# One hybrid decoder layer on one core: eight gate tiles placed in other groups of the SSD stage

## The chip, the cores and the metric

The kernel runs on 1 core of a Trainium2 chip, in one launch. The metric is device time in microseconds; a lower one is better. TensorE does the matmuls into PSUM, VectorE and ScalarE the elementwise work, GpSimd small copies, and SyncE and ScalarE issue the DMAs, each in its own order.

## The reference, cut to what matters

A layer takes 512 prompt tokens and 64 sample tokens (8 streams of 8), makes one wide input projection, and runs three branches whose outputs are merged with gates:

```python
hn = _rmsnorm(x, norm_g)
proj = hn @ w_in
u, v, gate_a, z, xbc, dt_raw, q, gate_x, merge = jnp.split(proj, _split_points(IN_SIZES), axis=-1)
...
h_a = u * _gmlp_spatial(v, w_spatial, b_spatial) * jax.nn.silu(gate_a)
xbc, conv_new = _causal_conv(xbc, conv0, conv_w, conv_b)
xs, bm, cm = jnp.split(xbc, [D_INNER, D_INNER + SSD_GROUPS * SSD_STATE], axis=-1)
...
y, h_new = _ssd(xh, dt, a, bm, cm, h0)      # chunks of 128 tokens, 8 groups of 4 heads
h_b = _gated_group_rmsnorm(y + xh * d_skip, z, ssd_norm_g)
...
m = g_a * (h_a @ w_proj_a) + g_b * (h_b @ w_proj_b) + g_x * (h_x @ w_proj_x)
return x + m @ w_out, ...
```

`gate_a` has 1024 channels, 8 tiles of 128. It is used only in branch A, which comes after the SSD stage.

## The kernel before, in words

All activations lie with channels on the partitions and the 576 tokens along the free dimension, in two halves of 288. Every float32 matmul is made of three fp32r terms: a weight block is split (`wsplit`, L100 and L101: a cast on ScalarE, a subtraction on VectorE) into `whi` and `wlo`, and `gemm_half` (L169) runs hi x hi, hi x lo and lo x hi over 8 blocks of channels, 24 matmuls of 288 columns for one tile and half, into one of four accumulators in PSUM.

The SSD stage works on 8 groups. A **job** is one tile of a projection with three parts: `load` (a DMA of weights on SyncE, two jobs ahead, into one of two slots of 1 MB), `prep` (the split, one job ahead), and `half(f)` for the two halves. One half with what follows it is called a **unit** here. The kinds of job:

- `conv_job(g, ci)`: a tile of xBC of group g; after its second half come the four taps of the convolution and SiLU on VectorE and ScalarE (L414 to L442).
- `z_job(g, j)`: z's two tiles of group g; tanh on ScalarE into a tile `th` of two buffers (L472), a product on VectorE into `zs` (L473), which has one buffer.
- `gate_job(jj)`: tile jj of `gate_a`; tanh (L743), product (L744) into a tile of its own that borrows a buffer of another name (`xs`, `raw`, `cacc`, `C`), and one store of 288 KB to `g_scr` by ScalarE's queue (L746). Weights are loaded for two tiles at once.
- `proj_job(r, p)`: branch B's output projection over a quarter of h_b.

Between the units stand the **steps** of the group whose convolutions were done a group before: twelve lists 0 to 11 of small matmuls and what goes with them (`steps`). Step 0 has the scores C·B of chunk 0 (`chunk_cb`, L541, L542), `start_y`, `decays(g, 2)` and the transposes of chunk 1 (`chunk_a`, L512); step 1 chunk 1's scores, the state of chunk 0 (`state`, L576, L582, L583) and, for the group before, `y_smp` (L614) and `gate_y` (L694 to L696 and the split into `qq`); step 3 chunk 2's scores, `y_off` (L601), `y_diag` (L557) of chunks 0 and 1, `decays(g, 3)` and `norm_y` of the group before (L708 to L711, L714); step 4 a state, `chunk_a(g, 3)` and `decays(g, 4)`; step 5 scores, `y_off` and `chunk_a(g, 4)`; step 8 the `y_diag` of chunks 2 and 3; step 9 that of the sample chunk and the transposes and updates of the sample states (`h0_T`, L653, L655; `h0_new`, L662, L667, L668); step 10 two `h0_T` and `c_h0` (L683); step 11 two `h0_new` and `c_h0`. `decays` loads a chunk's cumulative sums by a broadcast DMA into `e`, which has three buffers (L498), adds a mask on VectorE (L499) and takes exponentials on ScalarE (L501). All small results go through three PSUM buffers (`s_tile`).

`PLACES` says after which unit of its group each step stands; a place behind the group's last unit falls into the next group. `decays(g + 1, 0)` and `(g + 1, 1)` stand three units before the group's end, `chunk_a(g + 1, 0)` after its last unit, `conv_out(g + 1)` (eight small stores on ScalarE's queue, L450 to L454) after the next group's unit 3 or, from group 2 on, after the last unit.

TensorE's order is just the order of this list. The other engines' orders are set when the program is built, by a scheduler with costs of its own; each engine then works in order and waits for semaphores.

Before, groups 0 and 1 have 6 jobs, group 2 and all others 8; group 7, which has no next group, has gate tiles 0 to 3 where the others have convolutions. Tiles 4 to 7 follow in a tail with the last `y_smp`, `gate_y` and `norm_y`, then `proj_job(3, p)`.

Of the kernel before, what the change touches and what calls it, by code (L numbers as in the profile page):

```python
# [8 lines left out]
F32 = mybir.dt.float32  # L9
# [3 lines left out]
ALU = mybir.AluOpType  # L13
# [4 lines left out]
P = 128  # L18
D = 1024
KD = D // P  # L20
TP = 512
TS = 64
T = TP + TS
# [5 lines left out]
G = 8  # L29
# [4 lines left out]
TW = TP + 192  # L34
EPS = 1e-6
O_U, O_V, O_GA, O_Z, O_XBC, O_DT, O_Q, O_GX, O_M = 0, 1024, 2048, 3072, 5120, 9216, 9248, 9760, 10272
# [6 lines left out]
def tile_hybrid_step(  # L43
# [8 lines left out]
    V, S, PE, GP, SY = nc.vector, nc.scalar, nc.tensor, nc.gpsimd, nc.sync  # L52
# [3 lines left out]
    w_in2 = w_in[0]  # L56
# [7 lines left out]
    g_scr = dpool.tile([P, KD, T], F32, name="g_scr")  # L64
# [62 lines left out]
    def load_block(src, r0, nk, cols):  # L127

        raw = rpool.tile([P, 2048], F32, tag="wraw", name="wraw").rearrange("p (k c) -> p k c", k=nk)
        o = 0  # L130
        for c0, n in cols:
            SY.dma_start(out=raw[:, :, o:o + n],
                         in_=src[r0:r0 + nk * P, c0:c0 + n].rearrange("(k p) c -> p k c", p=P))
            o += n
        return raw

    def wsplit(raw, nk, o, n=P, e=None):
        hi = ws["pool"].tile([P, 1024], F32R, tag="whi", name="whi")[:, 0:nk * n].rearrange("p (k c) -> p k c", k=nk)
        lo = ws["pool"].tile([P, 1024], F32R, tag="wlo", name="wlo")[:, 0:nk * n].rearrange("p (k c) -> p k c", k=nk)
        split(raw[:, :, o:o + n], hi, lo, e)  # L140
        return hi, lo
# [48 lines left out]
    with ExitStack() as stb:  # L190
        banks(stb, 4, 1, 3)
        ws["pool"] = stb.enter_context(tc.tile_pool(name="wb", bufs=2))
        pb = stb.enter_context(tc.tile_pool(name="pb", bufs=1))
# [27 lines left out]
        for tiles in ((0, 1, 2), (3, 4)):  # L221
# [12 lines left out]
            w = 3 * P if n == 3 else P + TS  # L234
            for k in range(KD):
                ps = s_tile()
# [3 lines left out]
                g = gcol[:, k:k + 1]  # L240
# [480 lines left out]
        def gate_job(jj):  # L721

            k = {}

            def load():
                if jj % 2 == 0:
                    gate_th["w", jj // 2] = load_block(w_in2, 0, KD, [(O_GA + jj * P, 256)])

            def prep():
                k["w"] = wsplit(gate_th["w", jj // 2], KD, (jj % 2) * P)  # L730

            def half(f):
                if f == 0:
                    if jj < 3:
                        if jj == 0:
                            gate_th["x"] = pb.tile([P, 3, TW], F32, tag="xs", name="thx", bufs=2)
                        gate_th[jj] = gate_th["x"][:, jj, 0:T]
                    else:
                        tag, nb = (("raw", 2), ("raw", 2), ("cacc", 2), ("cacc", 2), ("C", 2))[jj - 3]
                        gate_th[jj] = pb.tile([P, T], F32, tag=tag, name="thm", bufs=nb)  # L740
                ps, sl = gemm_half(k["w"], KD, xh, xl, f)
                th = pb.tile([P, HT], F32, tag="th", name="th", bufs=2)
                S.activation(th, ps, AF.Tanh, scale=0.5)  # L743
                V.scalar_tensor_tensor(gate_th[jj][:, sl], th, 1.0, ps, ALU.add, ALU.mult)  # L744
                if f == 1:
                    S.dma_start(out=g_scr[:, jj], in_=gate_th[jj])  # L746
            return Job(load, prep, half)

        def proj_job(r, p):
# [25 lines left out]
        with tc.manual_schedule(engines={mybir.EngineType.PE}):  # L775
            def group_jobs(g):

                c = [conv_job(g + 1, ci) for ci in range(4)] if g + 1 < G else [gate_job(0), gate_job(1), gate_job(2), gate_job(3)]
                z = [z_job(g, 0), z_job(g, 1)]
                if g == 0:  # L780
                    return [z[0], *c, z[1]]
                if g == 1:
                    return [c[0], c[1], z[0], c[2], c[3], z[1]]
                if g == 2:
                    return [c[0], c[1], z[0], z[1], c[2], proj_job(0, 0), c[3], proj_job(0, 1)]
                p = [proj_job(g // 2 - 1, 2 * (g % 2) + i) for i in range(2)]
                a, b = (p, z) if g % 2 else (z, p)
                return [c[0], a[0], c[1], a[1], c[2], b[0], c[3], b[1]]

            def yd(g, *cs):  # L790
                y_add(g, cs, y_diag(g, cs))

            def steps(g):

                w = [[] for _ in range(12)]
                w[0] = [lambda: chunk_cb(g, 0), lambda: start_y(g), lambda: decays(g, 2), lambda: chunk_a(g, 1)]
                w[1] = [lambda: chunk_cb(g, 1), lambda: state(g, 0)]
                if g > 0:
                    w[1] += [lambda: y_smp(g - 1), lambda: gate_y(g - 1)]
                w[2] = [lambda: state(g, 1), lambda: chunk_a(g, 2)]  # L800
                w[3] = [lambda: chunk_cb(g, 2), lambda: y_off(g, 1), lambda: yd(g, 0, 1), lambda: decays(g, 3)]
                if g > 0:
                    w[3] += [lambda: norm_y(g - 1)]
                w[4] = [lambda: state(g, 2), lambda: chunk_a(g, 3), lambda: decays(g, 4)]
                w[5] = [lambda: chunk_cb(g, 3), lambda: y_off(g, 2), lambda: chunk_a(g, 4), lambda: h0_load(g, 0)]
                w[6] = [lambda: state(g, 3), lambda: chunk_t4(g), lambda: h0_load(g, 1)]
                w[7] = [lambda: y_off(g, 3), lambda: chunk_cb(g, 4)]
                w[8] = [lambda: yd(g, 2, 3), lambda: state_out(g), lambda: h0_T(g, 0, 0)]
                w[9] = [lambda: yd(g, 4), lambda: h0_T(g, 0, 1), lambda: h0_new(g, 0, 0), lambda: h0_new(g, 0, 1)]
                w[10] = [lambda: c_h0(g, 0), lambda: h0_T(g, 1, 0), lambda: h0_T(g, 1, 1)]  # L810
                w[11] = [lambda: h0_new(g, 1, 0), lambda: h0_new(g, 1, 1), lambda: c_h0(g, 1)]
                return w

            halves = [(j, h) for j in (conv_job(0, ci) for ci in range(4)) for h in range(2)]
            between = {}

            def put(u, *fs):
                between.setdefault(u, []).extend(fs)  # L820

            put(7, lambda: decays(0, 0), lambda: decays(0, 1))
            PLACES = {0: (3, 4, 5, 6, 7, 8, 9, 10, 11, 12, 13, 14), 1: (1, 3, 4, 5, 6, 7, 8, 9, 10, 12, 13, 14),
                      2: (1, 3, 4, 5, 6, 7, 8, 9, 10, 11, 12, 13)}
            for g in range(G):
                u0 = len(halves)
                halves += [(j, h) for j in group_jobs(g) for h in range(2)]
                n = len(halves) - u0
                if g == 0:
                    put(u0 + 2, lambda: chunk_a(0, 0), lambda: conv_out(0))  # L830
                else:

                    between[u0 - 1] = between.get(u0 - 1, []) + [lambda g=g: chunk_a(g, 0)]
                w = steps(g)
                at = PLACES.get(g, (0, 1, 2, 4, 5, 7, 8, 9, 10, 12, 13, 14))
                for i, a in enumerate(at):
                    put(u0 + a, *w[i])
                if g + 1 < G:
                    put(u0 + n - 3, lambda g=g: decays(g + 1, 0), lambda g=g: decays(g + 1, 1))
                    put(u0 + n + (3 if g < 2 else -1), lambda g=g: conv_out(g + 1))  # L840
            units = []
            for u, x in enumerate(halves):
                units += [x, (None, between.get(u, []))]
            tail = {0: [lambda: y_smp(G - 1), lambda: gate_y(G - 1)], 4: [lambda: norm_y(G - 1)]}
            for i, u in enumerate([(j, h) for j in (gate_job(jj) for jj in range(4, 8)) for h in range(2)]):
                units += [u, (None, tail.get(i, []))]
            units += [(j, h) for j in (proj_job(3, p) for p in range(4)) for h in range(2)]

            jobs = [u[0] for u in units if u[0] is not None and u[1] == 0]
            at = {id(j): i for i, j in enumerate(jobs)}  # L850
            jobs[0].load()
            jobs[0].prep()
            jobs[1].load()
            for j, h in units:
                if j is None:
                    for w_ in h:
                        w_()
                    continue
                i = at[id(j)]
                if h == 0:  # L860
                    if i + 2 < len(jobs):
                        jobs[i + 2].load()
                    if i + 1 < len(jobs):
                        jobs[i + 1].prep()
                j.half(h)
# [651 lines left out]
```

## Time and profile before

| | |
|---|---|
| median of 3 runs | 1118.99 us (1118.35 to 1119.67) |
| the profiled execution | 1120.8 us |
| its span, first to last instruction | 1119.1 us |
| TensorE, VectorE, ScalarE, GpSimd busy | 1088.0, 797.0, 628.6, 25.0 us |
| group 0 (its units in the trace) | 62.01 to 109.73 us |
| group 1 | 109.73 to 168.44 us |
| group 2 | 168.44 to 240.97 us |
| groups 3 to 6 | 240.97 to 505.10 us |
| group 7 | 505.10 to 570.19 us |

The limits of the groups are the starts of the first matmul of their first job. A row of the timeline gives start, duration, engine, line, operation, tiles and shapes, and in brackets how long the engine had been idle and what ended that. A matmul's row lasts longer than the distance to the next one, since matmuls are pipelined.

### The profile page before, as it was taken

What the parts mean: (1) busy time and instruction counts of PE and PEld (TensorE: products, weight loads), DVE (VectorE), ACT (ScalarE), POOL (GpSimd) and SP (SyncE); (2) the same over time, 40 slices, a digit from 0 to 9 for tenths busy, and PEclk for the clock granted to TensorE, in tenths of its full rate; (3) what the DMA queues carried; (4) which work ended last, traced back from release to release, by engine and by line L of the source; (5) the groups of instructions that cost most, each with busy time, mean ns of one, the idle gap of its engine ahead of it and who ended that gap; (6) DMA issues with size and microseconds to landing.
All of it is one profiled execution on the core that took longest, in us unless ns stands there. A gap on an engine that the chain in (4) does not pass through costs nothing. (4 is left out here: it accounts for less than half of the span.)

```text
span 1119.1 us, 20422 instructions
## 1 busy us (share of the span) xinstructions
PE 1088.0 (97%) x8152; PEld 1010.9 (90%) x8152; DVE 797.0 (71%) x1468; ACT 628.6 (56%) x1303; POOL 25.0 (2%) x109
## 2 busy tenths in 40 slices
PE   5999999999999999999999999999999999999997
PEld 3999889999999999999999777899999998889776
DVE  4779797868677886877644765899965567765743
ACT  6366686777767576775543345365643235565421
POOL 1010000000000000000000000000000000000000
PEclk9999999999999999999999999999999999999999
DMA  6343535344553525445235525744642543556311
GB/s 172 108 112 111 149 112 148 101 140 109 153 144 110 135 90 149 112 146 161 97 103 178 184 70 167 252 156 160 207 147 97 175 144 113 151 160 211 138 47 76
DMA packets 163214, 153.82 MB, mean 137 GB/s; under 512 B 10472, under 2 KB 141584, under 8 KB 163120
## 3 DMA queue, kind: packets, MB, share of 16 engines
q1 hardware_dynamic: 138288, 130.32, 38.4%
q10 hardware_dynamic: 24832, 22.21, 6.0%
q8 instruction: 64, 1.05, 0.4%
q14 instruction: 30, 0.25, 0.1%
HBM read 128.32 MB, written 24.18 MB: 136 GB/s over the span
## 5 line engine op out<-in xcount | busy, mean ns | idle before, releaser
L169 PE MATMUL acc<-hn_hi,whi 128*128 128x288 f32 x896 | 270.2, 302 | 0.2 <-DVE zs L473 0.2
L169 PE MATMUL acc<-hn_lo,whi 128*128 128x288 f32 x896 | 264.2, 295 | 0.0
L169 PE MATMUL acc<-hn_hi,wlo 128*128 128x288 f32 x896 | 264.1, 295 | 0.0
L169 PEld LDWEIGHTS acc<-hn_hi,whi 128*128 128x128 f32 x896 | 168.2, 188 | 2.3 <-issue 1.2
L169 PEld LDWEIGHTS acc<-hn_lo,whi 128*128 128x128 f32 x896 | 168.4, 188 | 0.4
L169 PEld LDWEIGHTS acc<-hn_hi,wlo 128*128 128x128 f32 x896 | 168.1, 188 | 0.1
L934 PE MATMUL acc<-hn_hi,w 128*128 128x288 f32 x640 | 110.1, 299 | 0.0
L934 PE MATMUL acc<-tT,w 128*128 128x288 f32 x720 | 107.0, 298 | 0.0
L100 ACT CAST w<-wraw 128x1024 fp32r<-128x1024 f32 x64 | 58.1, 916 | 87.0 <-PE acc L934 28.3
L101 DVE TENSOR_TENSOR wlo<-wraw,whi 128x1024 fp32r<-128x1024 f32 x72 | 87.9, 1221 | 23.0 <-ACT whi L100 22.3
L169 PE MATMUL acc<-hb,whi 128*128 128x288 f32 x512 | 104.2, 298 | 0.0
L934 PEld LDWEIGHTS acc<-tT,w 128*128 128x128 f32 x720 | 98.1, 188 | 1.2 <-issue 0.9
L100 ACT CAST whi<-wraw 128x1024 fp32r<-128x1024 f32 x72 | 75.6, 1050 | 41.6 <-PE acc L169 39.3
L934 PEld LDWEIGHTS acc<-hn_hi,w 128*128 128x128 f32 x640 | 92.5, 188 | 1.9 <-DVE thx L952 0.5
L428 DVE SCALAR_TENSOR_TENSOR cacc<-raw,cwh,cacc 128x600 f32<-128x600 f32 x96 | 80.5, 838 | 3.6 <-ACT cacc L426 2.7
L169 PEld LDWEIGHTS acc<-hb,whi 128*128 128x128 f32 x512 | 81.5, 188 | 0.6 <-issue 0.6
L101 DVE TENSOR_TENSOR w<-wraw,w 128x1024 fp32r<-128x1024 f32 x64 | 66.8, 1053 | 14.5 <-ACT w L100 14.2
L169 PE MATMUL acc<-hb,wlo 128*128 128x288 f32 x256 | 75.3, 294 | 0.0
L101 DVE TENSOR_TENSOR w<-S,w 128x1024 fp32r<-128x1024 f32 x40 | 48.9, 1221 | 26.9 <-ACT w L100 26.9
L100 ACT CAST w<-S 128x1024 fp32r<-128x1024 f32 x40 | 42.1, 1054 | 27.4 <-PE acc L156 18.4
L501 ACT ACTIVATE e<-e,nacs 128x128 f32<-128x128 f32 (+1 forms) x160 | 50.0, 383 | 11.1 <-DVE e L499 9.9
L934 PE MATMUL acc<-hn_lo,w 128*128 128x288 f32 x320 | 56.1, 295 | 0.0
(386 smaller groups left out, 2016.4 us busy)
## 6 DMA issues: line engine op xcount, KB each, us to landing
wraw<-in_w_in_dram SPq DMA_DIRECT2D x44, 1024.0 KB
wraw<-in_w_in_dram SPq DMA_DIRECT2D x16, 512.0 KB
e<-a_scr SPq DMA_DIRECT2D x32, 256.0 KB
h<-in_state_ssm_dram SPq DMA_DIRECT2D x16, 512.0 KB
out_dram<-h ACTq DMA_DIRECT2D x16, 512.0 KB
wraw<-in_w_proj_b_dram SPq DMA_DIRECT2D x8, 1024.0 KB
ebc<-e_scr SPq DMA_DIRECT2D x16, 288.0 KB
wraw<-in_w_mem_kv_dram SPq DMA_DIRECT2D x4, 1024.0 KB
```

The lines of the kernel that those rows point to most:

```text
L100: S.copy(hi, v)
L101: (e or V).tensor_tensor(lo, v, hi, ALU.subtract)
L169: PE.matmul(ps[:, 0:HT], lhsT=a[:, k], rhs=b(k)[:, sl], start=(n == 0), stop=(n == 3 * nk - 1))
L428: V.scalar_tensor_tensor(a[:, 0:n], raw[:, i:i + n], cwh[:, i, q:q + 1], a[:, 0:n], ALU.mult, ALU.add)
L501: S.activation(e[:, h, 0:w], e[:, h, 0:w], AF.Exp, bias=nacs[:, c, h0_ + h:h0_ + h + 1])
L934: PE.matmul(ps[:, 0:HT], lhsT=w[:, r, k], rhs=x(q, k), start=first and n == 0, stop=n == 11, skip_group_check=True)
```

## The change: which job stands where

Gate tile 0 becomes the last job of group 0, tile 1 the second job of group 1, tiles 2 and 3 stay in group 7, and 4 to 7 in the tail. Groups 0 and 1 have 7 jobs then, group 7 has 6. In group 0 z's second tile moves forward between the first two convolutions; in group 1 z's tiles keep their order. The steps of group 1 and of group 2 (the default places) begin at unit 0, those of group 7 stand one after each of its 12 units. Each gate tile loads its own weights (512 KB), its product is written into `th` in place, and each half is stored by itself.

```diff
             def load():
-                if jj % 2 == 0:
-                    gate_th["w", jj // 2] = load_block(w_in2, 0, KD, [(O_GA + jj * P, 256)])
+                k["raw"] = load_block(w_in2, 0, KD, [(O_GA + jj * P, P)])
 
             def prep():
-                k["w"] = wsplit(gate_th["w", jj // 2], KD, (jj % 2) * P)
+                k["w"] = wsplit(k["raw"], KD, 0)
 
             def half(f):
-                if f == 0:
-                    if jj < 3:
-                        if jj == 0:
-                            gate_th["x"] = pb.tile([P, 3, TW], F32, tag="xs", name="thx", bufs=2)
-                        gate_th[jj] = gate_th["x"][:, jj, 0:T]
-                    else:
-                        tag, nb = (("raw", 2), ("raw", 2), ("cacc", 2), ("cacc", 2), ("C", 2))[jj - 3]
-                        gate_th[jj] = pb.tile([P, T], F32, tag=tag, name="thm", bufs=nb)
                 ps, sl = gemm_half(k["w"], KD, xh, xl, f)
                 th = pb.tile([P, HT], F32, tag="th", name="th", bufs=2)
                 S.activation(th, ps, AF.Tanh, scale=0.5)
-                V.scalar_tensor_tensor(gate_th[jj][:, sl], th, 1.0, ps, ALU.add, ALU.mult)
-                if f == 1:
-                    S.dma_start(out=g_scr[:, jj], in_=gate_th[jj])
+                V.scalar_tensor_tensor(th, th, 1.0, ps, ALU.add, ALU.mult)
+                S.dma_start(out=g_scr[:, jj, sl], in_=th)
...
-                c = [conv_job(g + 1, ci) for ci in range(4)] if g + 1 < G else [gate_job(0), gate_job(1), gate_job(2), gate_job(3)]
+                c = [conv_job(g + 1, ci) for ci in range(4)] if g + 1 < G else [gate_job(2), gate_job(3)]
                 z = [z_job(g, 0), z_job(g, 1)]
                 if g == 0:
-                    return [z[0], *c, z[1]]
+                    return [z[0], c[0], z[1], c[1], c[2], c[3], gate_job(0)]
                 if g == 1:
-                    return [c[0], c[1], z[0], c[2], c[3], z[1]]
+                    return [c[0], gate_job(1), c[1], z[0], c[2], c[3], z[1]]
...
+                if g == G - 1:
+                    return [c[0], a[0], c[1], a[1], b[0], b[1]]
                 return [c[0], a[0], c[1], a[1], c[2], b[0], c[3], b[1]]
...
-            PLACES = {0: (3, 4, 5, 6, 7, 8, 9, 10, 11, 12, 13, 14), 1: (1, 3, 4, 5, 6, 7, 8, 9, 10, 12, 13, 14),
-                      2: (1, 3, 4, 5, 6, 7, 8, 9, 10, 11, 12, 13)}
+            PLACES = {0: (3, 4, 5, 6, 7, 8, 9, 10, 11, 12, 13, 14), 1: (0, 1, 2, 4, 5, 6, 8, 9, 10, 11, 12, 13),
+                      G - 1: tuple(range(12))}
```

## Rows read from the trace of the kernel before

**Rows 1.** The page, busy time of each engine.

```profile
PE 1088.0 (97%) x8152; PEld 1010.9 (90%) x8152; DVE 797.0 (71%) x1468; ACT 628.6 (56%) x1303; POOL 25.0 (2%) x109
```

**Rows 2.** Windows: groups 0, 1, 2, 3 to 6, and 7; columns in its head.

```profile
core 0: us, PE busy (x) PEld busy (x) DVE busy (x) ACT busy (x) POOL busy (x), PEclk, DMA share, GB/s
62.01:109.73 47.72, 47.72 (x381) 46.73 (x379) 40.40 (x84) 29.45 (x72) 3.28 (x14) 1.00 0.31 88
109.73:168.44 58.71, 54.36 (x443) 50.59 (x441) 47.75 (x94) 43.51 (x109) 2.15 (x11) 1.00 0.47 135
168.44:240.97 72.53, 70.88 (x595) 66.37 (x594) 54.34 (x105) 55.82 (x142) 2.15 (x13) 1.00 0.48 140
240.97:505.10 264.13, 262.79 (x2144) 252.54 (x2142) 206.40 (x404) 184.08 (x435) 7.88 (x40) 1.00 0.43 124
505.10:570.19 65.09, 65.09 (x535) 62.81 (x533) 40.99 (x80) 34.25 (x77) 0.00 (x0) 1.00 0.44 132
```

**Rows 3.** Timeline of TensorE in groups 1 and 2.

```profile
120.08 0.49 PE L541 MATMUL sps<-C,xs 128*128 128x128 f32 x2 [0.71 <-DVE h L668]
121.35 0.44 PE L512 MATMUL sps<-ident,xs 128*128 128x128 f32 x2 [0.78 <-DVE e L542]
...
130.59 0.66 PE L614 MATMUL sps<-ident,yos 128*128 128x128 f32 x4 [0.35 <-DVE e L542]
...
138.93 0.35 PE L601 MATMUL sps<-C,hT 128*128 128x128 f32 x1 [0.33 <-DVE hT L583]
...
141.91 0.40 PE L709 MATMUL acc<-qq,onesn 128*128 128x288 f32 x1 [0.94 <-DVE qq L101]
...
151.86 0.52 PE L512 MATMUL sps<-ident,xs 128*128 128x128 f32 x3 [1.20 <-DVE e L542]
...
178.86 0.55 PE L512 MATMUL sps<-ident,xs 128*128 128x128 f32 x3 [0.55 <-ACT h0T L655]
...
197.48 0.29 PE L708 MATMUL acc<-qq,onesn 128*128 128x288 f32 x1
197.61 0.29 PE L709 MATMUL acc<-qq,onesn 128*128 128x288 f32 x1
...
206.39 0.68 PE L601 MATMUL sps<-C,hT 128*128 128x128 f32 x4 [0.66 <-DVE hT L583]
```

**Rows 4.** Timeline of TensorE at the end of group 5.

```profile
438.92 0.55 PE L512 MATMUL sps<-ident,xs 128*128 128x128 f32 x3 [1.16 <-DVE h L668]
```

**Rows 5.** Timelines of VectorE and ScalarE in group 1.

```profile
118.74 0.69 DVE L499 TENSOR_TENSOR e<-e,tri 128x512 f32<-128x512 f32 x1 [3.23 <-DMA e<-a_scr]
...
136.43 0.71 ACT L430 ACTIVATE raw<-cacc 128x600 f32<-128x600 f32 x1 [5.46 <-DMA out_dram<-co]
```

**Rows 6.** The gate's lines, ns min/median/max, and the splits' groups, mean ns.

```profile
L743 ACT ACTIVATE th<-acc x16: 387/409/418, 509.3 to 597.6; 128x288 f32<-128x288 f32 x16
...
L744 DVE SCALAR_TENSOR_TENSOR thm<-th,acc x10: 443/446/454, 557.2 to 598.9; 128x288 f32<-128x288 f32 x10
...
L746 ACTq DMA_DIRECT2D g_scr<-thm x5: 326/346/346, 562.1 to 599.4; - x5
...
L101 DVE TENSOR_TENSOR wlo<-wraw,whi 128x1024 fp32r<-128x1024 f32 x72 | 87.9, 1221 | 23.0 <-ACT whi L100 22.3
...
L100 ACT CAST whi<-wraw 128x1024 fp32r<-128x1024 f32 x72 | 75.6, 1050 | 41.6 <-PE acc L169 39.3
```

**Rows 7.** Timelines of TensorE and VectorE in group 7.

```profile
512.74 0.60 PE L614 MATMUL sps<-ident,yos 128*128 128x128 f32 x4
...
519.76 0.76 DVE L101 TENSOR_TENSOR qq<-zs,qq 128x576 fp32r<-128x576 f32 x1
```

**Rows 8.** Windows: two loads of 512 KB, then one of 1 MB, columns as above.

```profile
450.00:454.00 4.00, 4.00 (x31) 3.90 (x30) 4.00 (x9) 1.94 (x3) 0.00 (x0) 1.00 1.13 297
524.00:528.00 4.00, 4.00 (x39) 3.71 (x39) 2.65 (x6) 3.51 (x6) 0.00 (x0) 1.00 1.06 330
```

## The prediction

> **What bounds the kernel now.** The page says that TensorE is busy 97% of the span [rows 1], so only TensorE's idle time can be won. The table of windows by group of the SSD stage, read next, shows where that is [rows 2]. Group 0 has TensorE busy 47.72 of 47.72 us, group 1 54.36 of 58.71, group 2 70.88 of 72.53, groups 3 to 6 together 262.79 of 264.13, and group 7 all of 65.09. The granted clock is 1.00, the 2.4 GHz level, in all of them. So the stage idles 4.35 us in group 1, 1.65 in group 2 and 1.34 in groups 3 to 6.
>
> A wait costs more than the idle shown, because a matmul's row lasts 0.29 us while the next starts 0.13 us later [rows 3]: each idle stretch hides another 0.16 us. The timeline of TensorE has ten waits in groups 1 and 2, the eight of [rows 3] and two short ones. They cost 6.00 us of idle and 10 x 0.16 = 1.6 us, 7.6 us in all. Groups 3 to 6 lose at most 2.0 us (1.34 and some 0.6 for the overlap), 0.5 per group, more than half of it in one wait [rows 4].
>
> Nearly all ten end with a VectorE instruction. VectorE's share of the time without those 7.6 us is (40.40 + 47.75 + 54.34) / 171.4 = 83% in groups 0 to 2, and 206.40 / 264.13 = 78% in groups 3 to 6 [rows 2]. These groups differ by density: 12 steps lie between 12 units in groups 0 and 1 and between 16 from group 2 on (a unit is half a job, 24 matmuls at 0.13 us, some 3.15 us).
>
> **Two waits look like VectorE but begin elsewhere.** At 118.74 VectorE had stood 3.23 us for the scores of a decay, and what was queued behind, the update of the states (L668), then held the PSUM tiles that TensorE wanted at 120.08 and 121.35 [rows 3, 5]. At 136.43 ScalarE had stood 5.46 us behind a store of conv_out [rows 5]. The square in gate_y came late by that, and so did the waits at 138.93 and 141.91, and the backlog at 151.86.
>
> **The change part by part.**
>
> TensorE's work stays the same: the same eight gate tiles, each two units. VectorE and ScalarE do the same per tile: a split of 1.05 us on ScalarE and 1.22 on VectorE, and two halves of 0.41 and 0.45 us [rows 6]. What moves is two tiles, from group 7 to groups 0 and 1: 12.6 us of TensorE, 2 x (1.22 + 0.90) = 4.2 us of VectorE, 2 x (1.05 + 0.82) = 3.7 us of ScalarE. Groups 0 to 2 then carry 146.7 us of VectorE in 184.0 us, 80% in place of 83%, near the 78% at which groups 3 to 6 lose 0.5 us each. Group 7 goes from 40.99 in 65.09 us (63%) to 36.8 in 52.5 (70%).
>
> The places of the steps do more than the share. Wait by wait, before and after:
> - 120.08 and 121.35: the step with decays (1, 2) came one unit after the step whose y_diag frees the score tile (units 12 and 13); now it comes two units after (12 and 14). That is over 3.15 us of slack against 3.23 us of waiting. But step 11 of group 0 (two h0_new) now falls on the same unit as step 0 of group 1, and its four PSUM tiles go through three buffers. Nothing before shows just this; by the nearest rows it costs between nothing and what these two waits cost now, 0.71 + 0.78 + 2 x 0.16 = 1.8 us. I take the middle, 0.9.
> - 130.59: conv_out and step 1 wanted four PSUM tiles of three in one unit. Step 1 now stands at unit 1, conv_out alone at unit 3.
> - 138.93: y_off followed state by one unit, now by two.
> - 141.91: norm_y follows gate_y by three units in place of two, and conv_out's stores no longer come just behind the store of the sample states.
> - 151.86: step 5 still follows step 4 by one unit, so this one may stay in part.
> - 178.86: group 1's step 10 and group 2's step 0 shared a unit; now group 1's steps end inside it.
> - 206.39 and the two short ones, in group 2: with the default places step 5 comes two units after step 4, and gate_y two units earlier than z needs its tile.
>
> For what is left I take the 0.5 us of a group from 3 to 6, in groups 1 and 2, with bounds of nothing (as group 0 now) and 2.3 (group 2 now: 1.65 and four times 0.16).
>
> Group 7 loses its four empty units: a step after each of 12. The tightest chain is gate_y to norm_y, three units before and two now. In the profile y_smp's transposes start at 512.74 and the last half of qq is ready at 520.52, 7.8 us later [rows 7]. Two units give 6.3 us, and the small matmuls of two steps 2 x 1.2 (65.09 less 16 units of 3.15, over 12 steps), 8.7 us in all, so it fits by 0.9 us. I take 0.5 us for group 7, bounds nothing and group 1's loss of now, 4.35 + 6 x 0.16 = 5.3.
>
> The other edits cost nothing on the path:
> - The output goes into the tanh tile, which a store now holds. Two tiles turn round every two units (6.3 us), and only the gate tiles of the tail follow each other. The tanh, product and issue take 0.41 + 0.45 + 0.35 [rows 6]. Even 5 us for a store to land would leave TensorE three more PSUM buffers.
> - Eight more stores on ScalarE's queue issue for 0.35 us each, 2.8 us on an engine that is busy 74% at the densest [rows 2, 6]. Each waits for VectorE's product, and behind it ScalarE's copies out of PSUM wait. The cover is the four accumulators; a rival below prices its loss.
> - Four loads of 1 MB become eight of 512 KB on SyncE's queue, each with a slot of its own. All slots are free one or two jobs ahead, since no pair of tiles holds one any longer than a job. Two loads of 512 KB moved with a broadcast at 297 GB/s, one of 1 MB with small loads at 330 [rows 8], so 512 KB take 1.8 us of a lead of 6.3.
>
> The Trainium skill speaks against that last edit: "DMA: Bandwidth & Descriptors", section Bandwidth, wants loads of 1 MiB or more, and its fit of 2.0 us plus bytes at 436 GB/s makes two halves 6.4 us against 4.4, an estimate of 8 us over the four pairs if loads were the path. By that the sum would end at 1121.8 us; by [rows 8], which differ by 10%, at the price of the last rival.
>
> **The sum.** 0.9 + 0.5 + 0.5 + 0.5 = 2.4 us stay of 7.6, so 5.2 us go. The profiled execution took 1120.8 us (span 1119.1), which becomes 1115.6. The median of the runs is 1.8 us lower, 1118.99, and becomes 1113.8. A measurement tells some 0.2%, 2.2 us, from no change.
>
> **The rivals.**
> - *The waits only move* (0.18). VectorE's work is not less, and it is served in order, so a backlog from two convolutions in a row (group 2 opens with them) meets other steps. For it: group 2, at 16 units, still loses 2.3 us. Against it: groups 3 to 6 have the same work and lose 0.5. If groups 0, 1 and 2 each lose 2.3 us and group 7 0.5, the gain is 0.2 us: 1118.8.
> - *The dense last group gives it back* (0.06, the slower side). With no unit free of a step, one delay would pass from step to step through the PSUM tiles. At the 0.76 us that a wait costs now (7.6 over 10), 12 steps lose 9.1 us; against 5.7 won elsewhere that is 3.4 us slower, 1122.4. It decides slower from 7.9 us lost in group 7, 0.66 per step. Against it: no convolution runs there, VectorE stands at 70%, and the group idles nothing today.
> - *The stores block ScalarE* (0.08). If each of the two moved gates repeats what conv_out's stores did at 136.43, the waits behind that (0.33 + 0.94 + 1.20 + 3 x 0.16 = 2.95 us) come twice: 5.9 against 5.2, 1119.7. Against it: a gate issues one store per 3 us, conv_out eight in a row.
> - *More than forecast* (0.06). All 7.6 us go, and some of the 2.0 in groups 3 to 6, whose long wait of 1.16 us [rows 4] also comes through L668: below 1110.8.
> - *The small loads come late* (0.02). Were the gates' 4.2 MB on the path, 297 in place of 330 GB/s would cost 14.1 - 12.7 = 1.4 us: 1115.2. Against it: the leads above.
>
> **How the numbers follow.** The forecast has 0.60, with its own range from 1110.8 (the 7.6 us and a little of groups 3 to 6) to 1116.5 (2.5 us won, the upper bounds of the boundary and of one group). The first rival ends the range at 1118.8; beyond it lie the last group, most of the blocked stores and a tail of the first, 0.17 with the low end. Faster by over 0.2% (below 1116.8) is 0.60 + 0.06 + 0.02 and 0.05 of the first rival, 0.73. Within 0.2%: 0.13 of the first and 0.06 of the others, 0.19. Slower: 0.08, most of the last group and a part of the stores.
>
> **What would show it.** In the profile after: TensorE's idle in groups 1 and 2 falls from 6.00 us to about 1; no wait for qq or for L668 of over 0.5 us remains at the start of group 1 or before norm_y; group 0 and group 1 are longer by 6 to 7 us less their waits, and group 7 is shorter by 12 to 12.6. The prediction is wrong if group 7 idles over 2 us, if VectorE again stands over 3 us for scores at a group's start with TensorE waiting behind it, or if ScalarE stands behind a gate's store.

## The result: 0.7% slower, and the profile after

The changed kernel takes 1126.97 us (median of 4 runs, 1125.09 to 1128.65), the kernel before 1119.31 in runs beside it: ratio 1.0068, interval 1.0057 to 1.0080, some 7.7 us slower. The forecast was 1113.8 us, 5.2 us faster, and its range ended at 1118.8. The profiled execution took 1125.09 us, its span 1123.4. The traces of before (1120.8 us) and after are 4.3 us apart, and what follows accounts for these 4.3; no trace shows the other 3.4 of the 7.7 us.

The page's busy times answer [rows 1]:

```profile
PE 1090.0 (97%) x8152; PEld 1014.7 (90%) x8152; DVE 797.0 (71%) x1468; ACT 634.5 (56%) x1307; POOL 25.3 (2%) x109
```

VectorE has exactly the time it had. ScalarE has 5.9 us more and four instructions more; nothing in the diff adds arithmetic there. The windows of groups 0, 1, 2, 3 to 6, and 7 answer [rows 2]:

```profile
core 0: us, PE busy (x) PEld busy (x) DVE busy (x) ACT busy (x) POOL busy (x), PEclk, DMA share, GB/s
60.74:118.47 57.73, 57.56 (x467) 55.45 (x465) 47.24 (x94) 37.21 (x95) 4.61 (x16) 1.00 0.33 90
118.47:186.56 68.09, 62.34 (x509) 58.86 (x507) 48.97 (x97) 48.60 (x113) 2.10 (x11) 0.97 0.50 142
186.56:259.44 72.88, 68.99 (x540) 65.72 (x538) 50.92 (x97) 52.48 (x124) 2.19 (x11) 0.95 0.40 117
259.44:521.88 262.44, 262.19 (x2144) 252.61 (x2142) 205.85 (x404) 184.24 (x436) 6.93 (x40) 1.00 0.44 127
521.88:574.17 52.29, 52.29 (x439) 50.01 (x437) 36.21 (x75) 31.44 (x72) 0.00 (x0) 1.00 0.41 117
```

Group 7 did what was forecast: 12.8 us shorter, without idle. Groups 3 to 6 won 1.7 us. What was lost lies in groups 0 to 2: they take 198.70 us in place of 178.96. The two gate tiles account for 12.6 of that and the old waits, 7.6, could have gone, so a loss-free stage would take 184.0; 14.7 us are lost there, where the forecast left 1.9. TensorE's idle in them is 0.17 + 5.75 + 3.89 = 9.8 us. Its timeline has these waits of over 0.7 us in groups 1 and 2, against [rows 3]:

```profile
124.13 0.55 PE L512 MATMUL sps<-ident,xs 128*128 128x128 f32 x3 [0.78 <-DVE e L542]
...
154.29 0.87 PE L512 MATMUL sps<-ident,xs 128*128 128x128 f32 x3 [4.72 <-ACT BT L520]
...
222.49 0.61 PE L169 MATMUL acc<-hn_hi,whi 128*128 128x288 f32 x1 [2.47 <-ACT whi L100]
...
224.12 0.61 PE L169 MATMUL acc<-hn_hi,wlo 128*128 128x288 f32 x1 [0.78 <-DVE wlo L101]
```

The waits of [rows 3] are nearly all gone, as forecast. Two long ones have come, and both end with ScalarE. What made ScalarE late stands in its timeline of group 1 (an ACTq row is a DMA issue on its queue; BT is a tile of transposes that `chunk_a` has copied out of PSUM):

```profile
136.96 0.40 ACT L734 ACTIVATE th<-acc 128x288 f32<-128x288 f32 x1
137.26 0.26 ACT L450 COPY co<-sps 108x128 f32<-108x128 f32 x1
137.54 0.27 ACTq L453 DMA_DIRECT2D out_dram<-co  x1
...
138.60 0.36 ACTq L736 DMA_DIRECT2D g_scr<-th  x1
138.99 0.40 ACTq L454 DMA_DIRECT2D out_dram<-co  x1
140.30 0.25 ACTq L453 DMA_DIRECT2D out_dram<-co  x1
141.34 0.31 ACTq L454 DMA_DIRECT2D out_dram<-co  x1
142.33 0.25 ACTq L453 DMA_DIRECT2D out_dram<-co  x1
142.73 0.31 ACTq L454 DMA_DIRECT2D out_dram<-co  x1
143.08 0.40 ACT L414 COPY raw<-acc 128x288 f32<-128x288 f32 x1 [4.59 <-DMA g_scr<-th]
143.49 1.28 ACT L710 ACT_TABLE_LOAD   x1
144.79 0.41 ACT L710 ACTIVATE rs<-acc 128x288 f32<-128x288 f32 x1
145.20 1.28 ACT L501 ACT_TABLE_LOAD   x1
146.50 1.28 ACT L501 ACTIVATE e<-e,nacs 128x128 f32<-128x128 f32 x4
147.80 1.28 ACT L710 ACT_TABLE_LOAD   x1
149.09 0.41 ACT L710 ACTIVATE rs<-acc 128x288 f32<-128x288 f32 x1
149.40 0.34 ACT L418 COPY raw<-acc 128x224 f32<-128x224 f32 x1
149.76 1.28 ACT L711 ACT_TABLE_LOAD   x1
...
153.93 0.26 ACT L520 COPY BT<-sps 128x128 f32<-128x128 f32 x1
```

Two things follow each other. First conv_out's eight stores (L453, L454), which issue in 0.3 us each: the fifth, sixth and seventh come 1.0 to 1.3 us after the one ahead of them, and the accumulator copy behind the eight has stood 4.59 us. Then norm_y: its two logarithms (L710) have exponentials of decays(1, 3) between them, and each change between logarithm and exponential costs a table load of 1.28 us, four where the kernel before had two:

```profile
141.69 1.28 ACT L710 ACT_TABLE_LOAD   x1
142.99 0.71 ACT L710 ACTIVATE rs<-acc 128x288 f32<-128x288 f32 x2
143.72 1.28 ACT L501 ACT_TABLE_LOAD   x1
```

BT is copied 11 us after the stores let go, and TensorE waits for it. Group 2 shows both too: ScalarE stands 4.89 us behind conv_out's stores, and loads tables at 210.89, 212.61, 215.21 and 216.93. In the kernel before it stood 2.90 us at the same place, and VectorE ended that. First the changed kernel, then the kernel before:

```profile
209.86 0.70 ACT L430 ACTIVATE raw<-cacc 128x600 f32<-128x600 f32 x1 [4.89 <-DMA out_dram<-co]
```

```profile
191.38 0.70 ACT L430 ACTIVATE raw<-cacc 128x600 f32<-128x600 f32 x1 [2.90 <-DVE cacc L428]
```

Behind each long idle stretch TensorE runs slower. The windows of two stretches after them:

```profile
155.00:157.00 2.00, 2.00 (x10) 2.00 (x10) 2.00 (x3) 2.00 (x4) 0.00 (x0) 0.50 0.00 0
225.00:228.50 3.50, 3.50 (x16) 3.50 (x16) 3.38 (x8) 1.25 (x4) 0.00 (x0) 0.50 0.00 0
```

The granted clock is 0.50, the 1.2 GHz level, and the matmuls start 0.24 us apart where they start 0.13 apart before and after. About ten matmuls in group 1 and twenty in group 2 did so, an estimated 1.1 and 2.2 us. TensorE's busy time agrees: in groups 0 to 2 it grew from 172.96 to 188.89 us, 3.3 more than the 12.6 of the two tiles.

### The profile page after: what moved, and what is told of

Same layout as the page of the kernel before. It is cut to its first block, busy times and chain, and to the rows that moved or that the text cites. A ratio compares the mean times of both kernels' runs of the same rounds, so it can differ in the third digit from the quotient of the medians.

```text
span 1123.4 us, 20456 instructions
## 1 busy us (share of the span) xinstructions
PE 1090.0 (97%) x8152; PEld 1014.7 (90%) x8152; DVE 797.0 (71%) x1468; ACT 634.5 (56%) x1307; POOL 25.3 (2%) x109
## 3 DMA queue, kind: packets, MB, share of 16 engines
q8 instruction: 64, 1.05, 0.4%
```

## The experiments

All times of groups in one table: length in us and, in brackets, TensorE's idle (length less its busy time), from the windows; "loads" is the number of table loads of norm_y in groups 1 and 2. Each ratio is to the kernel before on the same chip.

| kernel | ratio, interval | group 0 | group 1 | group 2 | loads |
|---|---|---|---|---|---|
| before | 1 | 47.72 | 58.71 (4.35) | 72.53 (1.65) | 2, 2 |
| changed | 1.0068, 1.0057 to 1.0080 | 57.73 | 68.09 (5.75) | 72.88 (3.89) | 4, 4 |
| e1 logarithms together | 1.0022, 1.0012 to 1.0032 | 58.07 | 69.68 (6.58) | 67.30 (0.98) | 2, 2 |
| e2 conv_out a group end earlier | 1.0004, 0.9990 to 1.0018 | 58.13 | 66.32 (4.72) | 69.41 (3.01) | 2, 4 |
| e3 all these stores on GpSimd | 0.9998, 0.9986 to 1.0010 | 57.83 | 62.96 (1.95) | 70.59 (2.98) | 2, 4 |
| e4 before, new gate job | 1.0000, 0.9989 to 1.0012 | 47.72 | 58.37 (3.99) | 72.54 (1.65) | 2, 2 |
| e5 e3 and other places | 0.9955, 0.9937 to 0.9973 | 57.93 | 62.12 (1.05) | 70.34 (2.42) | 2, 2 |
| e6 group 2's old places | 1.0041, 1.0026 to 1.0056 | 58.35 | 69.59 (6.12) | 69.85 (2.97) | 4, 2 |
| e7 before, conv_out on GpSimd | 1.0055, 1.0036 to 1.0074 | 47.72 | 61.20 (5.60) | 73.34 (2.75) | 2, 2 |
| e8 before, two more loads per group | 1.0081, 1.0065 to 1.0097 | 47.72 | 62.73 (6.55) | 76.65 (4.34) | 4, 4 |
| e9 e5, norm_y later in group 2 | 0.9935, 0.9923 to 0.9947 | 58.29 | 61.42 (0.63) | 65.53 (0.00) | 2, 2 |
| e10 e5, norm_y early in group 2 | 0.9946, 0.9933 to 0.9958 | 57.71 | 61.34 (0.52) | 67.68 (1.41) | 2, 4 |
| e11 gates' stores on GpSimd | 1.0055, 1.0042 to 1.0068 | 58.14 | 67.00 (4.39) | 72.42 (3.69) | 4, 4 |
| e12 conv_out's on GpSimd | 0.9998, 0.9990 to 1.0007 | 57.49 | 63.73 (2.73) | 70.38 (2.93) | 2, 4 |
| e13 e12, two more loads in group 1 | 1.0037, 1.0025 to 1.0049 | 57.52 | 66.85 (4.08) | 70.73 (3.08) | 4, 4 |
| e14 e7, one order put back | 1.0046, 1.0029 to 1.0063 | 47.72 | 59.34 (5.19) | 74.44 (3.79) | 2, 2 |

### The gate job by itself (e4)

The kernel before with only the first hunk of the diff: loads of 512 KB, halves stored one by one, the product in place; jobs and places as before.

> The kernel before with the new gate job alone (loads of one tile, product in place, a store per half), all jobs and steps where they were. Store theory in its strong form (twice the gate's stores cost by themselves): 1 to 3 us slower than before, 1120 to 1122. If the loss needs the new places: within 1 us of before, 1118 to 1120. The last would also clear the loads of 512 KB.

Ratio 1.0000, and the groups are within 0.4 us of those of before. Where the tiles stood before, the gate job's code costs nothing. The Trainium skill's rule for loads of 1 MiB or more ("DMA: Bandwidth & Descriptors", section Bandwidth) shows no price here. By the Trainium skill's fit of 2.0 us a load plus its bytes at 436 GB/s (the same page, section Anatomy of one DMA — SWDGE (gpsimd) path) eight loads of 512 KB in place of four of 1 MB would be an estimated 8 us slower, were they the path.

### Table loads (e1, e6, e8)

e1 holds the exponentials of decays(g, 3) in groups 1 and 2 behind norm_y's second logarithm (the core of its edit):

```diff
-                S.activation(e[:, h, 0:w], e[:, h, 0:w], AF.Exp, bias=nacs[:, c, h0_ + h:h0_ + h + 1])
+                x = S.activation(e[:, h, 0:w], e[:, h, 0:w], AF.Exp, bias=nacs[:, c, h0_ + h:h0_ + h + 1])
+                if h == 0 and after:
+                    run(x, after())
```

> The changed kernel, with the exponentials of decays(g, 3) in groups 1 and 2 held behind the second logarithm of norm_y: two table loads in each of the two groups in place of four. Table theory (the two extra loads, 2.6 us of ScalarE per group, made the long waits at 154 and 219 to 224 us): most of the loss of 7.7 us goes, 1119 to 1121 us, and no wait of TensorE over 2 us stays in groups 1 and 2. Store theory (ScalarE stood behind conv_out's and the gate's stores): the stores block as before, at most 2 us go, 1125 to 1127.

e6 gives group 2 its old places, with norm_y at unit 5 in place of 4:

```diff
-                      G - 1: tuple(range(12))}
+                      2: (1, 3, 4, 5, 6, 7, 8, 9, 10, 11, 12, 13), G - 1: tuple(range(12))}
```

> The changed kernel with group 2's list of places as before the change (step 0 at unit 1 and so on); all else changed. Table theory: norm_y's two Ln of group 2 follow each other again, two table loads in place of four there, group 2 falls from 72.9 to 67 to 69 us, group 1 keeps its loss (68 to 70): 4 to 5.5 us below the changed kernel, ratio 1.002 to 1.003. Rival (the prediction's step: the default places help group 2, and its loss is what group 1 leaves behind): group 2 at 72 or above, ratio 1.006 to 1.009.

e8 is the kernel before with a one-column exponential between the two logarithms of norm_y(0) and norm_y(1) (the core of its edit):

```diff
-                S.activation(rs[:, sl], ms[:, 0:HT], AF.Ln)
+                ln = S.activation(rs[:, sl], ms[:, 0:HT], AF.Ln)
+                if g < 2 and f == 0:
+                    ex = S.activation(lnx[:, 0:1], ones[:, 0:1], AF.Exp)
+                    run(ex, ln)
+                elif ex is not None:
+                    run(ln, ex)
```

> The kernel before with one exponential of a column of 128 values put between the two Ln of norm_y in groups 1 and 2 (its output is not used): four table loads for norm_y in place of two, in each of the two groups, and nothing else of the change. Table theory: each group's norm_y comes 2.6 us later, y_smp and z wait for it: groups 1 and 2 each 1 to 3 us longer, ratio 1.002 to 1.005. Rival (table loads are covered by ScalarE's idle time, the loss of the changed kernel needs its stores or its shorter distance of conv_out and norm_y): groups 1 and 2 as before within 0.5 us, ratio 1.000.

e1 took 5.6 us out of group 2 and nothing out of group 1: there the wait for BT stayed (5.33 us at 157.31), since the stores still held ScalarE 4.65 us and the copy of BT came behind a convolution's SiLU. Its 1123.34 us lie between the two forecasts. e6 took 3.0 us out of group 2; with norm_y two units behind gate_y TensorE waits 1.32 us for `qq` there, so the old places trade one wait for another, and 69.85 us lie between its two forecasts as well. e8 is the plainest: two more loads in each of two groups, and the kernel before becomes 0.8% slower, 9 us. Its ScalarE in group 1, where L713 is the logarithm and L715 the added exponential:

```profile
141.06 1.28 ACT L713 ACT_TABLE_LOAD   x1
142.36 0.41 ACT L713 ACTIVATE rs<-acc 128x288 f32<-128x288 f32 x1
142.79 1.28 ACT L715 ACT_TABLE_LOAD   x1
144.08 0.20 ACT L715 ACTIVATE lnx<-ones 128x1 f32<-128x1 f32 x1
144.30 1.28 ACT L713 ACT_TABLE_LOAD   x1
145.60 0.41 ACT L713 ACTIVATE rs<-acc 128x288 f32<-128x288 f32 x1
146.02 1.28 ACT L501 ACT_TABLE_LOAD   x1
```

Side by side the second logarithm would start at about 142.66 (two of them take 0.71 us together where they stand so); it starts 2.9 us later. Group 1 grows by 4.0 us and group 2 by 4.1, more than the forecast of either theory (1 to 3): TensorE idles 2.2 and 2.7 us more, and the clock drops as well, for the windows show a granted clock of 0.97 and 0.98 where the kernel before has 1.00. The Trainium skill's rule to group functions by table set and finish one set before switching ("ScalarE: Activation LUTs", section Rules for kernel authors) agrees with these rows. The Trainium skill names, in the same section, one set for exp and ln together, with one load in place of two. These rows show a load of 1.28 us at each change between the two, and they decide.

### The stores (e2, e3, e11, e12, e13)

e2 puts conv_out of groups 1 and 2 behind the last unit of the group before, four units ahead of its place:

```diff
-                    put(u0 + n + (3 if g < 2 else -1), lambda g=g: conv_out(g + 1))
+                    put(u0 + n - 1, lambda g=g: conv_out(g + 1))
```

e3 issues conv_out's and the gates' stores from GpSimd; e11 does so for the gates' alone, e12 for conv_out's alone; e13 is e12 with e8's exponential in group 1. The core of e3 (e11 is its last pair of lines, e12 its first two pairs):

```diff
-                S.dma_start(out=conv_p[0, 0, :, c0:c0 + P], in_=co[27 * ci:27 * ci + 3])
-                S.dma_start(out=cso[:, c0:c0 + P], in_=co[27 * ci + 3:27 * ci + 27])
+                GP.dma_start(out=conv_p[0, 0, :, c0:c0 + P], in_=co[27 * ci:27 * ci + 3])
+                GP.dma_start(out=cso[:, c0:c0 + P], in_=co[27 * ci + 3:27 * ci + 27])
...
-                S.dma_start(out=g_scr[:, jj, sl], in_=th)
+                GP.dma_start(out=g_scr[:, jj, sl], in_=th)
```

> The changed kernel, with conv_out of groups 1 and 2 after the last unit of the group before, as in the later groups, so no longer one unit ahead of norm_y. ScalarE's order then has two table loads in group 1, still four in group 2. Store theory: ScalarE's waits of 4.6 and 4.9 us ahead of norm_y go, and with them both long waits of TensorE: 1117 to 1120 us. Table theory: only group 1's long wait goes (4.9 us and about 1 us of halved clock), 1120 to 1122; group 2 keeps its 4 us.

> The changed kernel, with conv_out's and the gate's small stores issued by GpSimd in place of ScalarE. ScalarE has two table loads in group 1, still four in group 2. Store theory: ScalarE never stands behind a small store any more, the SSD stage loses under 3 us to waits: 1112 to 1117 us, below the kernel before. Table theory: group 2 keeps its wait of 3 to 4 us: 1118 to 1122.

> The changed kernel with only the gates' stores issued by GpSimd; conv_out's eight stay on ScalarE. The prediction's rival (the gate's own stores block ScalarE): group 1 loses most of its idle (68.1 to 63 to 65 us), ratio 1.001 to 1.004. Other theory (what blocks is the eight stores of conv_out that now stand beside the gate's tile and its loads; the gate's two only add to them): group 1 stays at 67 us or above, ratio 1.005 to 1.008.

> The changed kernel with only conv_out's stores issued by GpSimd; the gates' sixteen stay on ScalarE. If conv_out's stores are what blocks ScalarE: group 1 as in e3, 63 us, and two table loads there, ratio 0.999 to 1.002. If the gate's stores are: group 1 stays at 66 us or above, ratio 1.004 to 1.008. If both have to be gone, e11 and e12 both stay above 1.003.

> e12 (conv_out's stores on GpSimd) with one exponential of a column of 128 values between the two Ln of norm_y in group 1 (its output is not used): the stores stay off ScalarE, the four table loads of the changed kernel come back in group 1 alone. If both causes count in group 1: its length goes from 63.7 to 65 to 68 us, ratio 1.001 to 1.004. If in group 1 the stores are the whole cause: 63.2 to 64.5 us, ratio 0.999 to 1.001.

e3 and e12 agree within 0.0001 of the ratio: with conv_out's stores off ScalarE, and the pair of logarithms of group 1 together by the order that came with it, all that was lost against before is won back, and the gates' stores add nothing to that. It is no more than that: e3, at 1120.78 us, came out in the range of the table theory, and e2, at ratio 1.0004, at the border of the two, since group 2 keeps its four loads and some 3 us of idle in both. e11 confirms it from the other side: with the gates' stores gone ScalarE still stands behind conv_out's,

```profile
144.46 0.40 ACT L414 COPY raw<-acc 128x288 f32<-128x288 f32 x1 [5.24 <-DMA out_dram<-co]
```

and the time stays at 1.0055. In e12 the gate's store is issued between two copies and nothing waits behind it:

```profile
139.38 0.33 ACTq L736 DMA_DIRECT2D g_scr<-th  x1
140.32 0.40 ACT L414 COPY raw<-acc 128x288 f32<-128x288 f32 x1 [1.02 <-PE acc L169]
140.73 1.28 ACT L710 ACT_TABLE_LOAD   x1
142.47 0.71 ACT L710 ACTIVATE rs<-acc 128x288 f32<-128x288 f32 x2 [0.46 <-PE acc L709]
143.20 1.28 ACT L711 ACT_TABLE_LOAD   x1
```

e12 also had the logarithms side by side in group 1, so e13 parts the two: stores off, four loads back. Group 1 grows from 63.73 to 66.85 us and the ratio from 0.9998 to 1.0037. Both causes count in group 1. e13 also prices the stores by themselves: it has the four loads of the changed kernel in both groups, and differs from it by 0.0031 of the ratio, in the traces 1.2 us in group 1 and 2.2 in group 2. The price is that of the move with the orders that the scheduler made of it; no run held all other orders fixed. e2 shows the third way round: ScalarE still stands 2.57 and 4.05 us behind conv_out's stores (in group 1 for the eight issues themselves, none of which is late), but farther from norm_y, with two loads in group 1, and most of the loss goes. Group 1 keeps 4.72 us of idle there.

### Both mended (e5, e9, e10)

e5 is e3 with places that put the logarithms together: step 5 of group 1 one unit later, group 2's list as before the change:

```diff
-            PLACES = {0: (3, 4, 5, 6, 7, 8, 9, 10, 11, 12, 13, 14), 1: (0, 1, 2, 4, 5, 6, 8, 9, 10, 11, 12, 13),
-                      G - 1: tuple(range(12))}
+            PLACES = {0: (3, 4, 5, 6, 7, 8, 9, 10, 11, 12, 13, 14), 1: (0, 1, 2, 4, 5, 7, 8, 9, 10, 11, 12, 13),
+                      2: (1, 3, 4, 5, 6, 7, 8, 9, 10, 11, 12, 13), G - 1: tuple(range(12))}
```

e9 and e10 are e5 with other places for group 2:

```diff
-                      2: (1, 3, 4, 5, 6, 7, 8, 9, 10, 11, 12, 13), G - 1: tuple(range(12))}
+                      2: (0, 1, 2, 5, 6, 7, 8, 9, 10, 12, 13, 14), G - 1: tuple(range(12))}
...
+                      2: (0, 1, 2, 4, 5, 6, 8, 9, 10, 12, 13, 14), G - 1: tuple(range(12))}
```

> The changed kernel with conv_out's and the gates' stores issued by GpSimd (as in e3), and with the steps of groups 1 and 2 placed so that both Ln of norm_y follow each other on ScalarE: step 5 of group 1 one unit later, group 2's list as before the change. Theory (ScalarE late by stores and by table loads): two table loads per norm_y in both groups, none of ScalarE's waits for a store; group 1 as e3 or below (62.9 us, idle under 2), group 2 as e1 (67.3 to 68.5, idle under 1.5); that is 2 to 4 us below e3, 1116.8 to 1118.8 on the chip of e3, ratio 0.996 to 0.998. Rival (VectorE's share and the dense places, not ScalarE): as e3, ratio 1.000, group 2 at 70 us or above.

> e5 with one thing changed: group 2 gets the places 0, 1, 2, 5, 6, 7, 8, 9, 10, 12, 13, 14, so that gate_y comes at unit 1, conv_out at unit 3 and norm_y at unit 5 (e5: gate_y 3, norm_y 5). In e5's trace TensorE waits 0.74 + 1.31 us for qq in norm_y of group 2 and then runs 16 matmuls at the half clock (1.7 us more). Theory (that is the distance from gate_y to norm_y, two units of 3.15 us, which is too short in group 2 with two convolutions in a row): with four units the wait is gone, group 2 falls from 70.35 to 67 to 68 us, ratio 0.993 to 0.995. Rival (ScalarE's and VectorE's work is as late there whatever the place): group 2 at 70 or above, ratio as e5, 0.9955 or above.

> e5 with one thing changed: group 2 gets the changed kernel's places but for step 5, at unit 6 in place of 7 (gate_y at unit 1, norm_y at unit 4, one behind conv_out as in the changed kernel). Two table loads per norm_y in ScalarE's order, stores on GpSimd. Table and store theory: norm_y one unit behind conv_out costs nothing by itself, since neither stores nor table loads stand between: group 2 at 67 to 68.5 us, ratio 0.993 to 0.9955. Rival (norm_y beside conv_out is itself too dense for VectorE): group 2 at 70 or above, ratio above 0.9955.

e5 is faster than both kernels, but group 2 kept 70.34 us, where its rival put it, though not at the rival's ratio of 1.000: with gate_y two units ahead of norm_y TensorE waits for `qq` again. e9, with four units between them, has no idle in group 2 and takes 65.53 us, less than forecast. All of TensorE's waits in its groups 0 to 2, by the list of waits (us in total, times, longest):

```profile
PE sps L662 <- ACT h0T L655: 0.6, 1, 0.6
PE sps L576 <- DVE e L542: 0.3, 1, 0.3
PE sps L512 <- DVE h L668: 0.2, 1, 0.2
```

e9's median is 1113.83 us against 1121.02 of the kernel before on the same chip, 7.2 us faster. e10 was to have two loads in group 2 and had four: its expectation on that was wrong, so it does not test what it was made for. It still came to 67.68 us there, 2.9 less than e3 with the same four loads and the same stores on GpSimd. The two differ only in the place of step 5, one unit earlier in group 2 and one later in group 1; that part of the loads is covered by this was not shown.

### The kernel before without those stores (e7, e14)

e7 puts conv_out's stores of the kernel before on GpSimd. e14 adds a hold of the eight exponentials of decays(1, 0) and (1, 1) behind the copy of BT (the core of its edit):

```diff
+                    if g == 1:
+                        between[u0 - 1] += [lambda: exps(1, 0, st_[1]["bt", 0]), lambda: exps(1, 1, st_[1]["bt", 0])]
```

> The kernel before with conv_out's stores issued by GpSimd in place of ScalarE, nothing of the change. Store theory: ScalarE's wait of 5.46 us behind a store in group 1 is gone and with it part of the waits behind it (0.33 + 0.94 + 1.20 us and the overlap, 2.95 at most): group 1 falls from 58.4 to 55.5 to 57.5 us, ratio 0.997 to 0.999. Rival (in the kernel before, ScalarE's waits behind stores were covered): group 1 at 58 or above, ratio 1.000. If the ratio is under 0.996, what e3 won was not the change's own loss alone.

> e7 (the kernel before with conv_out's stores on GpSimd) with the eight exponentials of group 1's first two decays held behind the copy of BT, as they stood in the kernel before; in e7 they had come ahead of it and TensorE waited 2.63 us for that copy. If e7 was slower by that order alone and the stores cost the kernel before too: group 1 at 55.5 to 57.5 us (before 58.4), ratio 0.996 to 0.999. If the stores were covered in the kernel before: 58 to 59 us, ratio 1.000. At or above e7's 61.2 us the order was not its cause.

Both are slower than the kernel before, against the expectation. ScalarE no longer waits for a store in either, but the scheduler that orders the other engines had answered with another order. In e7 the copy of BT came behind eight exponentials that wait for a broadcast:

```profile
114.33 2.45 ACT L501 ACTIVATE e<-e,nacs 128x128 f32<-128x128 f32 x8 [2.40 <-DVE e L499]
116.68 0.24 ACT L520 COPY BT<-sps 128x128 f32<-128x128 f32 x1
```

and TensorE waited 2.63 us for it at 116.97. In e14 that copy is ahead of them, but VectorE's products that release it (L528 the last) stand behind two masks, the first of which waits for that broadcast, and TensorE waits 1.77 us for the copy:

```profile
113.35 0.69 DVE L499 TENSOR_TENSOR e<-e,tri 128x512 f32<-128x512 f32 x1 [2.08 <-DMA e<-a_scr]
113.96 0.42 DVE L525 TENSOR_TENSOR xdt<-sps,dt 128x256 f32<-128x256 f32 x1
114.29 0.68 DVE L499 TENSOR_TENSOR e<-e,tri 128x512 f32<-128x512 f32 x1
114.89 0.42 DVE L528 TENSOR_TENSOR xdd<-sps,wdec 128x256 f32<-128x256 f32 x1
```

Group 1 is 1.9 us shorter in e14 than in e7 (59.34 against 61.20), and still 0.6 longer than in the kernel before. So what the stores cost the kernel before by themselves was not measured. What the two show is that e9 is not faster for that move alone.

## Why the prediction was wrong, step by step

- **The bound and the place of the gain: right.** What could be won lay in groups 1 and 2. e9 has 0.63 us of idle in group 1 and none in group 2, and takes 185.2 us in groups 0 to 2, 6.3 less than before with the two tiles added, of the 7.6 that the prediction counted there; another 1.0 comes from groups 3 to 6.
- **VectorE's share, 83% against 80%: right and beside the point.** VectorE's busy time did not change, its waits in [rows 3] went, and the time rose.
- **120.08 and 121.35, taken at 0.9:** one wait of 0.78 us is left at 124.13. Right; the size, the middle between two bounds, is partly luck.
- **130.59, 138.93, 178.86, 206.39:** gone, or 0.3 us at most. Right.
- **136.43 and 141.91: the step that failed.** The prediction saw ScalarE stand 5.46 us behind conv_out's stores [rows 5], laid that to the store of the sample states just ahead of them, and counted it as gone. It stayed, 4.59 us in group 1, with the sample states' store 11.8 us ahead of the first of the eight, and group 2 got one of 4.89. Nor was that store the reason before (last paragraph of this section). The prediction also counted norm_y as safer, three units behind gate_y in place of two. But the same places put norm_y one unit behind conv_out in place of two, so the logarithms met the backlog, and their pair was broken up by exponentials: two more table loads in each group, which no line of the prediction has. e12 prices the stores and the loads of group 1 together at 0.0070 of the ratio; e13 parts that into 0.0031 for the stores and 0.0039 for the loads.
- **151.86, "may stay in part":** became 4.72 us (group 2's 222.49: 2.47). Here the two causes reach TensorE.
- **The edits that cost nothing: right where it was tried.** e4 shows it for the loads and the gate's code in their old places, e11 and e3 against e12 for the gate's own stores. One reading was off: ScalarE is busy 77% in group 2 (55.82 of 72.53 us in [rows 2]), not 74% at the densest; no term of the sum hangs on it.
- **Group 7, 0.5 us lost:** none. Right, and the rival of the dense last group is out.
- **The rivals.** "The stores block ScalarE" named the engine and the kind of wait, but it priced the gate's stores as the added evil; the ones that blocked were conv_out's, which the change didn't touch, only their neighbours. By its letter the sign "ScalarE stands behind a gate's store" came true (the release at 143.08), but with those stores gone ScalarE stood 5.24 us (e11). At 1119.7 it was also short by the table loads and the clock. "The waits only move" would have kept VectorE's waits; they went.
- **The half clock** was in no term. It costs an estimated 3.3 us of the 14.7 lost.

The sum closes: 9.8 us of idle, 3.3 of half clock, and for the overlap eight waits at the prediction's 0.16 us, 1.3, make 14.4 of the 14.7 us lost in groups 0 to 2.

What the stalled issues wait for stands in the trace. The DMA issues on ScalarE's and SyncE's queues name eight completion counters, taken in turn, and the late issues of conv_out each wait for the counter that they name. In group 1 those at 140.30, 141.34, 142.33 and 142.73 start 0.02 to 0.03 us after the last landing on it (140.28, 141.32, 142.30, 142.70). The first of these counters had been taken by the gate's store of 133.94, the second by a 512 KB load which SyncE had issued at 132.81, the others by conv_out's own first stores. In the kernel before, the issue at 135.72 follows the landing at 135.70 of a broadcast load that SyncE had issued at 131.71; the store of the sample states, issued at 128.61, had landed at 131.81. So an earlier transfer of either queue holds the issue. No run changed the counters, and why those transfers landed so late, 6.3 and 8.5 us after their issue, stays open.

## What to carry to other kernels

When a step moves, follow what it meets on every engine, not only on the one that the waits name now: a stall of 5 us on ScalarE with waits of 0.33 to 1.20 us of TensorE behind it had one of 4.72 us behind it when norm_y, with a chain behind it, came one unit nearer. Count the changes of function on ScalarE between steps that may interleave, since a pair of logarithms with an exponential between them costs two table loads more. And price a long idle stretch of TensorE above its length: behind those of 4.72 and 2.47 us the matmuls ran at half the clock.

## What the runs showed that was not expected

- A table load takes 1.28 us in every row, and the kernels change tables both from logarithm to exponential and back. Two more of them in each of two groups (e8) made 9 us of kernel time out of 5.1 us of loads.
- After idle stretches of 4.72 and 2.47 us, the granted clock was 0.50 for some ten and twenty matmuls.
- Moving conv_out's stores from one engine's queue to another reordered work on VectorE and ScalarE that doesn't touch them (e7, e14), and the sum was slower, 1.0055 and 1.0046.
